# A two-layer hybrid trunk in fp32: one moving operand for twenty more units, the scan's values in one PSUM bank, and the scan branch's gates ahead of its projections

## The chip, the cores and the metric

The kernel runs on one core of a Trainium2 chip. The metric is the time of one execution in device microseconds (us). The matrix engine is called PE (its weight loads PEld), the vector engine DVE, the scalar engine ACT, the general-purpose engine POOL, and SP is the engine that issues most transfers.

## The reference, cut to what matters

Two layers work on a residual stream of 256 tokens by 1024 channels. In each layer one input projection of the normalised stream feeds three token mixers (a state-space scan, attention in a sliding window with sinks and rotary positions, and forgetting attention); each has its own gate path and projection, the results are merged by sigmoid gates and projected back.

```python
h = rms_norm(x, norm_w[layer])
proj = jnp.einsum('bsd,de->bse', h, w_in[layer])
(a_xbc, a_z, a_dt, b_q, b_k, b_v, b_z,
 c_q, c_k, c_v, c_f, c_z, gates) = jnp.split(proj, split_at, axis=-1)
y_a = mamba2_branch(a_xbc, a_z, a_dt, ...)        # 4 groups of 4 heads, chunks of 128 tokens
y_b = sliding_window_branch(b_q, b_k, b_v, b_z, sinks[layer], cos, sin)
y_c = forgetting_attention_branch(c_q, c_k, c_v, c_f, c_z, f_bias[layer])
branch = jnp.einsum('bsiw,iwd->bsid', jnp.stack([y_a, y_b, y_c], axis=2), w_proj[layer])
g = jax.nn.sigmoid(gates.reshape(b, s, N_BRANCH, d) + gate_bias[layer])
x = x + jnp.einsum('bsd,de->bse', jnp.sum(g * branch, axis=2), w_out[layer])
```

Inside the scan branch, after the scan: `y = y + d_skip * xh`, then `y * silu(z)`, then an RMS norm over four groups of 256 channels. The sliding branch rotates q and k by `rope`. All inputs and the output are fp32.

## The kernel before, in words

**Precision.** Every dense product is made of three products of split operands: high by high, low by high, high by low. Weights arrive by SP's queue as `raw` tiles (6 buffers); ACT rounds them to `hi` (line 264) and DVE subtracts to get `lo` (line 265), four parts ahead of PE. The tokens `hT` stand split in the same way, transposed, with high and low side by side.

**Dense units.** A unit makes 128 output channels for all 256 tokens. There are two forms. `chan` (line 443) issues, for each of the 8 slices of the contraction, three matmuls of 256 columns into the same 256 columns of one PSUM bank. `chan_sum` (line 450) issues one of 512 columns, with high and low tokens as one moving operand, and one of 256 for the low weights; the two halves of the bank are then added by an ACT copy (line 463) and a DVE addition (line 464). `tok` makes token-major outputs for gates and projections.

**Who uses which form.** In `rotated` (line 499), which makes the rotary halves of k and q for the sliding branch, all units use `chan`, and DVE multiplies its PSUM result twice, by cosine and sine (line 508); POOL combines the halves (line 517). In `u_z` (line 807), the gate paths, branch 2 uses `chan_sum`, branches 0 (scan) and 1 (sliding) use `chan`.

**Background work.** Attention and scan are generators. `launch` puts one in a list with a delay, and after each dense unit `pump` runs the steps that are due by a planner's clock, within a budget, so that a run of small matmuls stands between two dense units. The constants `D_...` are these delays. PE's order is thus fixed as written; the order on DVE, ACT and POOL is a scheduler's. Dense units use 3 PSUM banks (`mm`), background work 5 (`mx`). A quad of attention heads takes four `mx` banks for its scores, then softmax, transposes of the probabilities (line 594) with ACT copies (line 599), then the product with v.

**The scan** (`ssd_group`, line 739; four groups per layer) has a last phase in which the values are made: for two chunks and two channel blocks, four outputs of 128 by 128, each in an `mx` bank of its own, each followed by a DVE operation that adds the skip term and writes the scan's output (line 801). Before it come the state product (copied by ACT, line 783) and two score products, by which DVE multiplies the decays (line 788). After it the generator waits `D_EVAC` and then returns a token that lets a later generator of the same kind start.

**The scan's group norm** (`group_norm`, line 844; four per layer) sums squares by a matmul with ones, computes the factor on DVE and POOL (line 852), writes it on the diagonals of two tiles by ACT (`diagonals`, line 867, four operations of 128 by 128), waits `D_GN2`, and broadcasts it with two matmuls (line 880). For the first three groups the diagonals are put in a list (`ends_later`), for the last they are written at once.

**The end of a layer** alternates units of gates (`gates_proj`, line 1163; `u_gate`, line 956, adds the bias and takes tanh) and of projections (`u_proj2`, line 990); `merge` (line 1002) takes a gate tile out of `y.gate` and multiplies. For branch 0 the order was four gate-path units, then gates 0, projection 0, gates 1, projection 1.

**SBUF** tiles come from pools by size: `L1` (256 fp32 per partition, 14 buffers), `L2` (512, 7 buffers), `L8` (2048).

Of the kernel before, what the change touches and what calls it, by code (L numbers as in the profile page):

```python
# [16 lines left out]
P = 128  # L17
# [5 lines left out]
EPS = 1e-6  # L23

D_SOFT, D_SOFT2, D_EVAC, D_SSD, D_SSD2 = 7.0, 3.0, 3.0, 8.0, 3.0
D_K, D_Q, D_QK, D_G0, D_FOX, D_BDMA, D_BIAS, D_BC = 6.0, 5.5, 2.0, 8.0, 0.0, 4.0, 2.6, 5.5
D_GN1, D_GN2, D_CUM, D_H, D_M = 6.0, 7.2, 12.0, (4.8, 6.4), 5.0
BUDGET = 1.35
T_PP, T_SSD, T_BIAS = 1, 1, 1
N_RAW, N_SPLIT = 6, 6  # L30
# [14 lines left out]
def hybrid_trunk(  # L45
# [29 lines left out]
    def pmx():  # L75
        return PS("mx", 5)
# [26 lines left out]
    def launch(br, gen, delay=0.0):  # L103
        clock["n"] += 1
        waiting.append([clock["t"] + delay, clock["n"], br, gen, None])
# [390 lines left out]

    def rotated(y, done):

        held = {}

        def u(half):
            def f(w):
                p = chan(y, w, half * P)
                for i in (half, 1 - half):
                    m = held[half, i] = T("L1", [P, S])
                    tt(halves(m), p, halves(cs[:, i, :]), op=ALU.mult)
                if half == 1:
                    done(held)  # L510
                pump()
            return f
        return u(0), u(1)
# [6 lines left out]
    def u_bk(y):  # L520

        def done(held):
            y.kT = T("L8", [P, 4, 2, S])
            add_rotated(y.kT[:, 0, :, :], held)
            for d in range(1, 4):
                m = 32 * d
                nc.gpsimd.dma_start(y.kT[m:P, d, :, :], y.kT[0:P - m, 0, :, :])
                nc.gpsimd.dma_start(y.kT[0:m, d, :, :], y.kT[P - m:P, 0, :, :])
        return rotated(y, done)

    def u_bq(y, g):

        def done(held):
            q = T("qt", [P, 2, S])
            add_rotated(q, held)
            launch(1, swa_quad(y, g, q), D_Q)
        return rotated(y, done)

    def attn_quad(pair, products, biases, nsink, v, vcols, sz, gated, scored=lambda: None):

# [198 lines left out]
    def ssd_group(y, g):  # L739
        yield lambda: not any(m[2] == 1 for m in waiting)  # L740
        yield "bcg"
        bcg = T("L4", [P, 4, S])
        nc.scalar.dma_start(bcg, y.cumd[4 * g:4 * g + 4, 0, :].partition_broadcast(P))
        yield D_BC
        yield "ssd"
        xdt = T("L2", [P, 2, 256])
        hs = slice(4 * g, 4 * g + 4)
        for t in range(2):
            p = pmx()
            for j in range(2):  # L750
                transpose(p[:, j * P:(j + 1) * P], y.xs[:, 2 * g + j, t * P:(t + 1) * P], ident)
            tt(xdt[:, t, :].rearrange("p (h d) -> p h d", h=4),
               p[:, 0:256].rearrange("p (h d) -> p h d", h=4), bc(y.dt[:, t, hs], 2, 64), op=ALU.mult)
        p = pmx()
        transpose(p[:, 0:P], y.bcT[:, g, 0:P], ident)
        bt = T("bt", [P, P])
        act(bt, p[:, 0:P], AF.Copy)
        ds = T("ds", [P, 4], bufs=2)
        tt(ds, bcg[:, :, P - 1], y.acum[:, 0, hs], op=ALU.subtract)
        act(ds, ds, AF.Exp)  # L760
        xds = T("L1", [P, 256])
        tt(xds.rearrange("p (h d) -> p h d", h=4), xdt[:, 0, :].rearrange("p (h d) -> p h d", h=4),
           bc(ds, 2, 64), op=ALU.mult)
        decs = []
        for c in range(2):
            tk = slice(c * P, (c + 1) * P)
            dec = T("L2", [P, 4, P])
            for h in range(4):
                stt(dec[:, h, :], bcg[:, h, tk], y.acum[:, c, 4 * g + h:4 * g + h + 1], negtri,  # L769
                    op0=ALU.subtract, op1=ALU.add)  # L770
            act(dec, dec, AF.Exp)
            decs.append(dec)

        cx = T("L2", [P, 4, P])
        act(cx, bcg[:, :, P:S], AF.Exp)
        tt(cx, cx, bc(y.bcT[:, 4 + g, P:S], 1, 4), op=ALU.mult)
        yield D_SSD
        tokens["bcg"] += 1

        p = pmx()  # L780
        mm(p[:, 0:256], bt, xds, start=True, stop=True)
        st = T("st", [P, 256])
        act(st, p[:, 0:256], AF.Copy)
        for c in range(2):
            tk = slice(c * P, (c + 1) * P)
            p = pmx()
            mm(p[:, 0:P], y.bcT[:, g, tk], y.bcT[:, 4 + g, tk], start=True, stop=True)
            tt(decs[c], decs[c], bc(p[:, 0:P], 1, 4), op=ALU.mult)
        yield D_SSD2
        for c in range(2):  # L790
            tk = slice(c * P, (c + 1) * P)
            for j in range(2):
                u = 2 * g + j
                py = pmx()
                for s in range(c + 1):
                    for i in range(2):
                        h = 2 * j + i
                        hc = slice(64 * h, 64 * h + 64)
                        a, b = (xdt[:, c, hc], decs[c][:, h, :]) if s == 0 else (st[:, hc], cx[:, h, :])
                        mm(py[64 * i:64 * i + 64, 0:P], a, b, start=(s == 0), stop=(s == c))  # L800
                stt(y.xs[:, u, tk], y.xs[:, u, tk], y.dsk[:, u:u + 1], py[:, 0:P],  # L801
                    op0=ALU.mult, op1=ALU.add)
        yield D_EVAC
        tokens["ssd"] += 1


    def u_z(y, br, u, c):
        def f(w):
            if u == 0 and br != 0:
                y.sz[br] = T("L8", [P, NK, S])  # L810
            if br == 2:
                o = y.sz[br][:, u, :]
                chan_sum(y, w, c, o)
                th = T("L1", [P, S])
                act(th, o, AF.Tanh, scale=0.5)
                y.zdone.add((br, u))
                stt(o, th, 1.0, o, op0=ALU.add, op1=ALU.mult)
                pump()
                return
            p = chan(y, w, c)  # L820
            if u == 0 and br == 0:
                y.yh[br] = T("L8", [P, 2, NK, P], F32R)
                y.yl[br] = T("L8", [P, 2, NK, P], F32R)
            th = T("L1", [P, S])
            finish(act(halves(th), p, AF.Tanh, scale=0.5))
            y.zdone.add((br, u))
            if br != 0:
                stt(halves(y.sz[br][:, u, :]), halves(th), 1.0, p, op0=ALU.add, op1=ALU.mult)
            else:
                drain(0)  # L830
                sz = T("L1", [P, S])
                stt(halves(sz), halves(th), 1.0, p, op0=ALU.add, op1=ALU.mult)
                tt(y.xs[:, u, :], y.xs[:, u, :], sz, op=ALU.mult)  # L833
                sq = T("L1", [P, S])
                act(sq, y.xs[:, u, :], AF.Square)
                y.sq.append(sq)
                if u % 2 == 1:
                    tt(y.sq[-2], y.sq[-2], y.sq[-1], op=ALU.add)

                    launch(3 if u < 4 else 4, group_norm(y, u // 2, y.sq[-2]), D_GN1 - (u == 7))  # L840
            pump()
        return f

    def group_norm(y, g, q0):
# [22 lines left out]
                    act(rb[:, t * P:(t + 1) * P], ident, AF.Copy, scale=v[:, 2 * t:2 * t + 1])  # L867


        if g < 3:  # L870
            ends_later.append(diagonals)
        else:
            diagonals()
        yield D_GN2
        if diagonals in ends_later:
            ends_later.remove(diagonals)
# [79 lines left out]
    def u_gate(y, br, c, t):  # L956

        def f(w):
            if t == 0:
                y.gb = T("L2", [P, 512])  # L960
                nc.scalar.dma_start(y.gb, gate_bias[y.l, br:br + 1, c:c + 512].to_broadcast([P, 512]))
            p = tok(y.hTh, y.hTl, w, t)
            g = T("L2", [P, 512])
            tt(halves(g), p, halves(y.gb), op=ALU.add)  # L964
            finish(act(g, g, AF.Tanh, scale=0.5))  # L965
            y.gate[t] = g
            pump()
        return f

# [30 lines left out]
        return f  # L1000

    def merge(y, br, c, t, p, keep=lambda f: f):
        g = y.gate.pop(t)
        m = y.mg[:, t, c:c + 512]
        if br == 1:
            stt(halves(m), halves(g), 1.0, p, op0=ALU.add, op1=ALU.mult)
        else:
            if br == 0:
                stt(halves(g), halves(g), 1.0, p, op0=ALU.add, op1=ALU.mult)
                gtt(m, m, g, op=ALU.add)  # L1010
            else:
                with tc.high_priority():
                    keep(stt)(halves(g), halves(g), 1.0, p, op0=ALU.add, op1=ALU.mult)
                    keep(tt)(m, m, g, op=ALU.add)
                launch(7 + t, mT(y, c, t), D_M)
# [120 lines left out]
    for y in layers:  # L1136
# [26 lines left out]
        def gates_proj(br):  # L1163
# [12 lines left out]
                    op(i, u_proj(y, br, c, 0), u_proj(y, br, c, 1))  # L1176
            seq = [(g, 0), (p, 0), (g, 1), (p, 1)]
            if br == 0:
                seq = [(lambda b: z1(C_ZA, 0, b), b) for b in range(4)] + seq
            return [lambda f=f, b=b: f(b) for f, b in seq]  # L1180

        if l == 0:
# [258 lines left out]
```

## Time and profile before

| | |
|---|---|
| median of 3 runs | 834.85 us (834.35 to 835.0) |
| profiled execution | 834.93 us |
| its span | 833.2 us |
| PE busy | 819.1 us (98%), 5941 matmuls |
| PEld busy | 748.3 us (90%) |
| DVE busy | 670.1 us (80%), 1482 instructions |
| ACT busy | 514.7 us (62%), 1062 instructions |
| POOL busy | 107.3 us (13%) |
| granted PE clock | 0.999 of full speed |

In a row of the timeline come the start in us, the length in us of what the row stands for, the engine, the line of the program, the operation, output and inputs by the program's names, the size, and `xN`, the number of instructions that it joins. In brackets stands how long the engine was idle before it and what ended that. In a row of the groups come busy time in us and the mean of one in ns. In a row of the waits come the total in us, the number of times and the longest. `L` stands for any tile of the pools L1 to L8, `pp` for softmax probabilities, `qt` for rotated or plain queries, `L97` is the helper that issues every matmul, `L101` the one that issues transposes.

### The profile page before, as it was taken

How to read it: one execution, taken by the hardware profiler on the slowest of the kernel's cores; microseconds unless marked ns; L12 is line 12 of the kernel's file. 1: busy time of each engine (PE TensorE's matmuls, PEld its weight loads, DVE VectorE, ACT ScalarE, POOL GpSimd, SP SyncE). 2: the span in 40 equal slices, each digit the busy share in tenths (PEclk: the TensorE clock that was granted, in tenths of full speed). 3: DMA queues.
4: the chain of work that ended last, by engine and by line, in shares of the span. 5: the costliest groups of instructions: out<-in, count | busy, mean ns of one | idle time of the engine just before them, and what ended most of it. 6: DMA issues, size and time to landing. Idle time of an engine off the chain costs nothing.

```text
span 833.2 us, 16124 instructions
## 1 busy us (share of the span) xinstructions
PE 819.1 (98%) x5941; PEld 748.3 (90%) x5941; DVE 670.1 (80%) x1482; ACT 514.7 (62%) x1062; POOL 107.3 (13%) x150
## 2 busy tenths in 40 slices
PE   8999999999999999999999999999999999999996
PEld 7999999988888998888999999989888889888896
DVE  6978998897987787865787789988889778786665
ACT  7747777665766676353564586766646667755442
POOL 3330010100111210210004200001002210121000
PEclk9999999999999999999999999999999999999999
DMA  9975554877656545776689455757776655476632
GB/s 298 273 208 166 174 164 148 241 214 222 173 156 187 169 140 164 246 237 201 209 262 264 133 166 177 205 162 215 230 202 178 176 157 156 133 238 216 215 102 75
DMA packets 129560, 159.41 MB, mean 191 GB/s; under 512 B 7970, under 2 KB 98202, under 8 KB 129482
## 3 DMA queue, kind: packets, MB, share of 16 engines
q1 hardware_dynamic: 114960, 140.53, 55.6%
q10 hardware_dynamic: 13690, 16.24, 6.5%
q0 software_dynamic: 832, 1.62, 0.7%
q8 instruction: 47, 0.77, 0.4%
q14 instruction: 31, 0.25, 0.1%
HBM read 154.63 MB, written 2.16 MB: 188 GB/s over the span
## 4 chain that ended last, share of the span: by engine, by line
PE 50%; DVE 6%; ACT 3%; issue 2%; POOL 1%; ACTq 0%; POOLq 0%; DVEq 0%
PE mm L97 45%; PE mx L97 3%; DVE lo L265 2%; PE mx L101 2%; ACT pp L568 1%; ACT L L867 1%; POOL sm L852 0%; ACT hi L264 0%; DVE pp L580 0%; DVE pp L562 0%; DVE L L833 0%; DVE L L259 0%; DVE L L769 0%; ACT L L599 0%; DVE lo L259 0%
## 5 line engine op out<-in xcount | busy, mean ns | idle before, releaser
L265 DVE TENSOR_TENSOR lo<-raw,hi 128x1024 fp32r<-128x1024 f32 (+2 forms) x276 | 313.5, 1154 | 66.4 <-ACT hi L264 56.7
L97 PE MATMUL mm<-L,hi 128*128 128x256 f32 (+1 forms) x1728 | 365.0, 302 | 0.0
L264 ACT ACTIVATE hi<-raw 128x1024 fp32r<-128x1024 f32 (+2 forms) x276 | 264.6, 980 | 96.3 <-PE mm L97 84.3
L97 PE MATMUL mm<-hi,L 128*128 128x512 f32 (+2 forms) x1232 | 323.7, 351 | 0.2
L97 PEld LDWEIGHTS mm<-L,hi 128*128 128x128 f32 x1728 | 278.4, 191 | 14.0 <-issue 3.4
L97 PE MATMUL mm<-L,lo 128*128 128x256 f32 x1056 | 281.7, 274 | 0.0
L97 PEld LDWEIGHTS mm<-hi,L 128*128 128x128 f32 x1232 | 216.9, 190 | 24.9 <-DVE L L265 1.0
L97 PE MATMUL mm<-lo,L 128*128 128x512 f32 (+2 forms) x616 | 213.6, 348 | 0.0
L97 PEld LDWEIGHTS mm<-L,lo 128*128 128x128 f32 x1056 | 202.5, 192 | 1.9
L97 PEld LDWEIGHTS mm<-lo,L 128*128 128x128 f32 x616 | 116.3, 190 | 11.5
L934 POOL TENSOR_SCALAR_AFFINE_SELECT bias<-bias 128x128 f32<-128x128 f32 x64 | 37.8, 626 | 397.2 <-DMA bias<-cumd 397.2
L568 ACT ACTIVATE pp<-pp,nm 128x128 f32<-128x128 f32 (+1 forms) x128 | 56.6, 444 | 19.0 <-DVE nm L562 19.0
L718 DVE SCALAR_TENSOR_TENSOR L<-L,vec,L 128x255 f32<-128x255 f32 (+2 forms) x96 | 46.1, 481 | 6.6 <-ACT L L715 5.2
L965 ACT ACTIVATE L<-L 128x512 f32<-128x512 f32 x24 | 15.1, 631 | 42.7 <-DVE L L964 42.7
L580 DVE TENSOR_SCALAR pp<-pp,rsum 128x128 f32<-128x128 f32 (+1 forms) x128 | 32.2, 315 | 0.5
L101 PE MATMUL mx<-ident,pp 128*128 128x128 f32 x192 | 27.4, 275 | 3.2 <-DVE L L801 3.2
L599 ACT ACTIVATE L<-mx 128x512 f32<-128x512 f32 x48 | 26.9, 594 | 0.0
L101 PEld LDWEIGHTS mx<-ident,pp 128*128 128x128 f32 x192 | 21.7, 141 | 5.4 <-DVE L L801 4.2
L722 ACT ACTIVATE L<-L 128x256 f32<-128x256 f32 x32 | 13.3, 417 | 20.8 <-DVE L L718 12.5
L562 DVE CUSTOM_DVE_ANT_0 pp<-mx,wmask,nsink 128x128 f32<-128x128 f32 x64 | 23.4, 413 | 1.4 <-PE mx L97 1.4
L568 ACT ACTIVATION_READ_ACCUMULATOR pp<-pp,nm 128x1 f32 x128 | 23.9, 187 | 0.0
L1010 POOL TENSOR_TENSOR L<-L,L 128x512 f32<-128x512 f32 x8 | 15.9, 1994 | 61.7 <-ACT hi L264 32.3
(202 smaller groups left out, 748.9 us busy)
## 6 DMA issues: line engine op xcount, KB each, us to landing
raw<-in_w_in_dram SPq DMA_DIRECT2D x191, 512.0 KB, 4.7
raw<-in_w_proj_dram SPq DMA_DIRECT2D x48, 512.0 KB, 5.4
raw<-in_w_out_dram SPq DMA_DIRECT2D x16, 512.0 KB, 5.5
bias<-cumd ACTq DMA_DIRECT2D x16, 256.0 KB, 4.0
L<-cumd ACTq DMA_DIRECT2D x8, 512.0 KB, 4.6
L<-in_gate_bias_dram ACTq DMA_DIRECT2D x12, 256.0 KB, 3.4
raw<-in_w_in_dram SPq DMA_DIRECT2D x4, 408.0 KB
raw<-in_w_in_dram SPq DMA_DIRECT2D x4, 384.0 KB
```

Of the source, the lines that this page charges most:

```text
L97: nc.tensor.matmul(o, a, b, **kw)
L101: nc.tensor.transpose(o, a, i)
L264: keep(act)(hi, src, AF.Copy)
L265: keep(tt)(lo, src, hi.bitcast(F32), op=ALU.subtract)
L562: nc.vector.tensor_tensor_reduce(out=pp[:, i, sl], in0=score(p, i, b), in1=biases(p, i, b), scale=-0.125, scalar=1.0e30 if ns is None else ...
L568: act(pp[:, i, sl], pp[:, i, sl], AF.Exp, scale=-1.0, bias=nm[:, e:e + 1], accum_out=sums[:, e:e + 1])
L580: ts(pp[:, i, sl], pp[:, i, sl], rs[:, 2 * i + b:2 * i + b + 1], 0.5, op0=ALU.mult, op1=ALU.mult)
L599: act(pT, pt, AF.Copy)
L718: stt(a[:, s:S], x_[:, 0:S - s], y.vec[:, 16 * j + u:16 * j + u + 1], a[:, s:S], op0=ALU.mult, op1=ALU.add)
L934: nc.gpsimd.affine_select(out=bias[:, i, dst], in_=bias[:, i, src], compare_op=ALU.is_ge, fill=NEG, base=0, pattern=[[-1, P]], channel_mul ...
L965: finish(act(g, g, AF.Tanh, scale=0.5))
L1010: gtt(m, m, g, op=ALU.add)
```

## The change

Three edits, with the delays that belong to them.

1. `rotated` gets a switch `both`; with it the unit goes through `chan_sum` into an `L1` tile and the two multiplications read that tile. It is on for query groups 1 to 3, off for group 0 and for k. `u_z` uses `chan_sum` also for branch 1 with `u < 4`.
2. The values of a scan group go into one bank: all products first, then two DVE operations of 256 columns in place of four of 128. The token comes back after `D_SSD3` = 1.0 in place of `D_EVAC` = 3.0.
3. In branch 0 both gate units come before both projection units, gate tiles are kept by column block and token block, all groups' diagonals go into the list, the first delay is the same for all groups, and `D_GN2` goes from 7.2 to 9.0.

```diff
-D_GN1, D_GN2, D_CUM, D_H, D_M = 6.0, 7.2, 12.0, (4.8, 6.4), 5.0
+D_GN1, D_GN2, D_CUM, D_H, D_M = 6.0, 9.0, 12.0, (4.8, 6.4), 5.0      # and D_SSD3 = 1.0
...
-    def rotated(y, done):
+    def rotated(y, done, both):
...
-                p = chan(y, w, half * P)
+                if both:
+                    p = T("L1", [P, S])
+                    chan_sum(y, w, half * P, p)
+                    p = halves(p)
+                else:
+                    p = chan(y, w, half * P)
...
-        return rotated(y, done)                # k
+        return rotated(y, done, False)
...
-        return rotated(y, done)                # q of group g
+        return rotated(y, done, g > 0)
...
         yield D_SSD2
+        py = pmx()
         for c in range(2):
-            tk = slice(c * P, (c + 1) * P)
             for j in range(2):
-                u = 2 * g + j
-                py = pmx()
+                o = py[:, S * j + P * c:S * j + P * c + P]
                 for s in range(c + 1):
                     for i in range(2):
...
-                        mm(py[64 * i:64 * i + 64, 0:P], a, b, start=(s == 0), stop=(s == c))
-                stt(y.xs[:, u, tk], y.xs[:, u, tk], y.dsk[:, u:u + 1], py[:, 0:P],
-                    op0=ALU.mult, op1=ALU.add)
-        yield D_EVAC
+                        mm(o[64 * i:64 * i + 64, :], a, b, start=(s == 0), stop=(s == c))
+        for j in range(2):
+            u = 2 * g + j
+            stt(y.xs[:, u, :], y.xs[:, u, :], y.dsk[:, u:u + 1], py[:, S * j:S * j + S], op0=ALU.mult, op1=ALU.add)
+        yield D_SSD3
...
-            if br == 2:
+            if br == 2 or br == 1 and u < 4:
...
-                    launch(3 if u < 4 else 4, group_norm(y, u // 2, y.sq[-2]), D_GN1 - (u == 7))
+                    launch(3 if u < 4 else 4, group_norm(y, u // 2, y.sq[-2]), D_GN1)
...
-        if g < 3:
-            ends_later.append(diagonals)
-        else:
-            diagonals()
+        ends_later.append(diagonals)
...
-            y.gate[t] = g
+            y.gate[c, t] = g
...
-        g = y.gate.pop(t)
+        g = y.gate.pop((c, t))
...
             if br == 0:
-                seq = [(lambda b: z1(C_ZA, 0, b), b) for b in range(4)] + seq
+                seq = [(lambda b: z1(C_ZA, 0, b), b) for b in range(4)] + [(g, 0), (g, 1), (p, 0), (p, 1)]
```

More of the change, by code (lines that the diff above doesn't have):

```diff
@@ L25 @@
 D_SOFT, D_SOFT2, D_EVAC, D_SSD, D_SSD2 = 7.0, 3.0, 3.0, 8.0, 3.0
-D_K, D_Q, D_QK, D_G0, D_FOX, D_BDMA, D_BIAS, D_BC = 6.0, 5.5, 2.0, 8.0, 0.0, 4.0, 2.6, 5.5
-D_GN1, D_GN2, D_CUM, D_H, D_M = 6.0, 7.2, 12.0, (4.8, 6.4), 5.0
+D_K, D_Q, D_QK, D_G0, D_FOX, D_BDMA, D_BIAS, D_BC, D_SSD3 = 6.0, 5.5, 2.0, 8.0, 0.0, 4.0, 2.6, 5.5, 1.0
+D_GN1, D_GN2, D_CUM, D_H, D_M = 6.0, 9.0, 12.0, (4.8, 6.4), 5.0
 BUDGET = 1.35
```

## The prediction, made before the changed kernel ran

> **What bounds the kernel now.** I read the first part of the profile page, then the waits view, and from there the timeline at the places that it names.
>
> ```profile
> span 833.2 us, 16124 instructions
> PE 819.1 (98%) x5941; PEld 748.3 (90%) x5941; DVE 670.1 (80%) x1482; ACT 514.7 (62%) x1062; POOL 107.3 (13%) x150
> PE mx L101 <- DVE L L801: 3.2, 4, 1.1
> PEld mx L97 <- ACT L L867: 2.4, 4, 0.8
> ```
>
> TensorE (PE) is busy for 98% of the span, so the time moves only with what PE has to do and with the few places where it stands still. Two of those places belong to this change: four waits of PE for line 801, the evictions of the scan's values (3.2 us in total, the longest 1.1), and four weight loads that wait for line 867, the diagonals of the scan branch's group norm. VectorE (DVE), at 80%, is the next engine; what is given to it must be watched.
>
> The profiled execution took 834.93 us, 1.73 more than its span, and the median of the runs is 834.85. The sum starts from 834.93; the two differ by 0.08, which is nothing here. I use 0.2% (1.7 us) as what a measurement of this kernel can tell from no change.
>
> **Twenty units with one operand.** A unit with `chan` issues 24 matmuls of 256 columns; one with `chan_sum` issues 8 of 512 and 8 of 256. Both forms already stand in the trace, in undisturbed stretches:
>
> ```profile
> 60.80 0.28 PE L97 MATMUL mm<-L,lo 128*128 128x256 f32 x1
> ...
> 66.16 0.28 PE L97 MATMUL mm<-L,lo 128*128 128x256 f32 x1
> 225.00 0.38 PE L97 MATMUL mm<-L,hi 128*128 128x512 f32 x1
> ...
> 226.97 0.38 PE L97 MATMUL mm<-L,hi 128*128 128x512 f32 x1
> ```
>
> In the first stretch 16 triples start within 66.16 − 60.80 = 5.36 us, 0.335 each, so eight triples, one unit, take 2.68 us. In the second, six pairs start within 1.97 us, 0.328 each, so a unit takes 2.62. The switch saves 0.06 us, because a column costs PE the same in either form and only eight starts are saved. The change switches 6 query units (groups 1 to 3, two each) and 4 gate units per layer, 20 in both layers: **−1.2 us**.
>
> [...]
>
> What the form adds runs on ACT and DVE:
>
> ```profile
> L463 ACT ACTIVATE qt<-mm 128x256 f32<-128x256 f32 x32 | 12.1, 377 | 16.4 <-PE mm L97 16.2
> L464 DVE TENSOR_TENSOR qt<-mm,qt 128x256 f32<-128x256 f32 x32 | 13.4, 419 | 2.9 <-ACT qt L463 2.5
> L508 DVE TENSOR_TENSOR L<-mm,cs 128x256 f32<-128x256 f32 x40 | 14.9, 413 | 0.6 <-PE mm L97 0.6
> 28.00:56.00 28.00, 28.00 (x251) 27.80 (x250) 25.13 (x42) 15.98 (x30) 11.70 (x15) 1.00 0.86 240
> 56.00:75.00 19.00, 19.00 (x190) 18.53 (x189) 14.81 (x46) 12.13 (x36) 3.14 (x6) 1.00 0.49 143
> ```
>
> Each unit gets one L463 (377 ns) and one L464 (419 ns). The PSUM bank is not held longer: it was read by two L508 of 413 ns, and now by 377 + 419. In the query stage (28 to 56 us) DVE is busy for 25.13 of 28 us and six more instructions bring 6 × 0.419 = 2.5 us per layer. That just fits into the 2.87 us left, and the weight splits stand ahead of PE by some units, so I take 0; without that cover it costs up to 2.5 per layer. The four gate units add 4 × 0.419 = 1.7 us per layer in the stage after it, where DVE is busy for 14.81 of 19 us: 0. (In both rows the columns are the stretch and its length, then the busy time of PE, PEld, DVE, ACT and POOL.)
>
> **The scan's values in one bank.** Each group now takes one bank where it took four, and two evictions of 256 columns where it made four of 128. What that ends can be seen where the transposes of a softmax follow the values in one run:
>
> ```profile
> 228.74 0.66 PE L101 MATMUL mx<-ident,pp 128*128 128x128 f32 x4
> 229.50 0.59 DVE L801 SCALAR_TENSOR_TENSOR L<-L,dsk,mx 128x128 f32<-128x128 f32 x2
> 229.89 0.44 PE L101 MATMUL mx<-ident,pp 128*128 128x128 f32 x2 [0.50 <-DVE L L801]
> 251.23 0.66 PE L101 MATMUL mx<-ident,pp 128*128 128x128 f32 x4
> 253.03 0.44 PE L101 MATMUL mx<-ident,pp 128*128 128x128 f32 x2 [1.14 <-DVE L L801]
> 636.98 0.66 PE L101 MATMUL mx<-ident,pp 128*128 128x128 f32 x4
> 638.13 0.44 PE L101 MATMUL mx<-ident,pp 128*128 128x128 f32 x2 [0.50 <-DVE L L801]
> 659.48 0.66 PE L101 MATMUL mx<-ident,pp 128*128 128x128 f32 x4
> 661.21 0.44 PE L101 MATMUL mx<-ident,pp 128*128 128x128 f32 x2 [1.07 <-DVE L L801]
> ```
>
> There are five banks for this work. The values hold four, the first four transposes take the fifth, and the last two need a bank that only L801 frees. Four transposes in 0.66 us, of which the last one's end is some 0.14 behind its pitch, set the next start at about +0.51. The fifth transpose started 1.15, 1.80, 1.15 and 1.73 us after the first: lost are 0.64, 1.29, 0.64 and 1.22, together **−3.8 us**. After the change the two generators also end up in different runs of PE (in the changed order no transposes follow the values directly), and even together they would need three banks. Both reasons take the wait away.
>
> The evictions get cheaper too. By the rows
>
> ```profile
> L801 DVE SCALAR_TENSOR_TENSOR L<-L,dsk,mx 128x128 f32<-128x128 f32 x32 | 9.2, 339 | 0.0
> L883 DVE SCALAR_TENSOR_TENSOR L<-L,vec,mx 128x256 f32<-128x256 f32 x16 | 6.9, 472 | 0.0
> ```
>
> 32 × 339 ns become 16 × 472: DVE gives back 3.3 us of what it got, off the path.
>
> [...]
>
> The delay before the group's token is given falls from 3.0 to 1.0. That lets later generators start sooner; what they run into is the first rival.
>
> **Gates first in the scan branch.** Both gate units now precede both projection units, the second delay of the group norm grows from 7.2 to 9.0, and the last group's diagonals are queued like the others. Before, two groups' broadcast products stood in one run, which stopped for the diagonals:
>
> ```profile
> 320.68 0.38 PE L97 MATMUL mm<-lo,L 128*128 128x512 f32 x1
> 321.47 0.39 PE L97 MATMUL mx<-L,ones 128*128 128x256 f32 x1 [0.41 <-ACT L L867]
> 322.05 0.62 PE L97 MATMUL mx<-L,ones 128*128 128x256 f32 x3 [0.20 <-ACT L L867]
> 728.84 0.38 PE L97 MATMUL mm<-lo,L 128*128 128x512 f32 x1
> 729.64 0.38 PE L97 MATMUL mx<-L,ones 128*128 128x256 f32 x1 [0.42 <-ACT L L867]
> 730.22 0.63 PE L97 MATMUL mx<-L,ones 128*128 128x256 f32 x3 [0.20 <-ACT L L867]
> ```
>
> From the start of the last dense matmul (its pitch is 0.22, read off 225.00 to 226.97 with 0.11 for the 256-column one) the first product should have come at 320.90 and 729.06. It came 0.57 and 0.58 late, and the next one 0.47 late again both times (0.58 instead of 0.11): 1.04 + 1.05 = **−2.1 us**. In the changed order every group's broadcast stands apart, at least one dense unit behind its own diagonals; that unit lasts over 2 us, the eight diagonals in two rows of 1.55 and 0.97 us about 2.5, and there are at least three units between the sums and the broadcast. The projections lose nothing, since they come two gate units later and their operand is ready sooner than needed. Four gate tiles live at once, which with the biases just fills the seven buffers of that size; the price if a gate unit had to wait for one is in the range.
>
> **Sum.** −1.2 − 3.8 − 2.1 = −7.1 us: 834.93 − 7.1 = **827.8 us**. Splitting the four joint runs adds a few switches, some tenths at most, and the runs without a wait are a little shorter than reckoned; I let these cancel.
>
> **The rivals.** First, a new wait takes the place of the old one. In the changed order four runs (groups 2 and 3, both layers) hold the scan's state product and its two score products directly ahead of a fox quad's scores. These take three banks, the scores four, so the third and fourth score bank wait for the copy of the state (L783) and the first L788. In the trace of before the same products were read late:
>
> ```profile
> 216.83 1.58 PE L97 MATMUL mx<-qt 64*128 64x128 f32 x16
> 221.06 0.59 PE L97 MATMUL mx<-L,bt 128*128 128x256 f32 x2
> 223.41 0.37 ACT L783 ACTIVATE st<-mx 128x256 f32<-128x256 f32 x1
> 223.46 0.68 DVE L788 TENSOR_TENSOR L<-L,mx 128x512 f32<-128x512 f32 x1
> 243.56 0.59 PE L97 MATMUL mx<-L,bt 128*128 128x256 f32 x2
> 246.39 0.36 ACT L783 ACTIVATE st<-mx 128x256 f32<-128x256 f32 x1
> 246.78 1.28 DVE L788 TENSOR_TENSOR L<-L,mx 128x512 f32<-128x512 f32 x2
> 250.75 1.22 DVE L265 TENSOR_TENSOR lo<-raw,hi 128x1024 fp32r<-128x1024 f32 x1
> ```
>
> The scores use a bank per 0.4 us (1.58 for four). The state and score products end some 0.8 us after 221.06, so a third bank would be wanted at about 222.7 and was free at 223.78 (1.1 late); in the other, wanted at 245.2, free at 246.75, and the fourth at 247.42 (1.7 late in all). With those lags the four runs cost 2 × 2.8 = 5.6 us and the time is 833.4, the gain nearly eaten. Against it: in both places L783 and L788 stood behind a softmax that was then in its queue; in the changed order only weight splits and one L464 precede them, and by their durations (at most 1.22 + 0.42 + 0.68 from the last score product) the wait is a few tenths, if any. I give the lags of before 0.12.
>
> Second, the slower side: the same wait, with one more weight split of 1.22 us ahead of L788 each time (DVE is busy for 80% of the span). Then the four cost 2 × (2.3 + 2.9) = 10.4, and the time is 838.2. It turns to slower by 0.2% from (7.1 + 1.7)/4 = 2.2 us per run on. 0.06, and 0.04 more for a wait of that size elsewhere.
>
> Third, DVE becomes the bound of the query stage and PE stands for all that was added: 2 × 2.5 = 5.0 us, 832.8. Against: the row above has just enough room. 0.07.
>
> Fourth, the change doesn't do what it says: the waits for banks and diagonals move a run further instead of going. Only the dense part stays: 833.7. The changed order speaks against it: 0.06.
>
> [...] The 48 units of that form in the trace run at 2.62: 0.01.
>
> **How the numbers follow.** The forecast has 0.64, between 826.2 (each of the eight stops also costs a weight load that otherwise runs beside a matmul, 748.3/5941 = 0.13 each and 1.0 in all, and the relief of DVE is worth some tenths) and 830.5 (the new bank waits at half their lags). The range of 826.2 to 833.2 takes in the third rival and half of the first; left out are the second, the fourth, the fifth and the other half, about 0.2. Faster by over 0.2% means under 833.2: 0.64 + 0.07 + 0.01 + half of 0.12 + most of what lies between, 0.82; same, the fourth and the rest of the first, 0.08; slower 0.10.
>
> **What would show it.** Right: no wait of PE for L801 or L867; 5781 matmuls instead of 5941; `chan_sum` units at 0.328 a pair; DVE near 670 + 5.0 + 3.4 − 3.3 = 675 us; the waits view of PE without those two names. Wrong: waits of PE for L783 or the changed L788 over 1 us (the first two rivals), waits of the query stage's matmuls for L265 (the third), or PE waiting for the diagonals again, now with a projection behind it.

## The result, and the profile after

The changed kernel took 830.0 us (median of 5 runs, 829.68 to 830.79) against 834.85 us before (5 runs, 833.68 to 835.57). The ratio is 0.9942, interval 0.993 to 0.9954: faster by 4.8 us, with 3.8 to 5.8 inside the interval. The forecast was 827.8 in a range of 826.2 to 833.2: the direction and the range held, and 2.2 us of the expected gain are missing.

The first part of the page of after:

```profile
span 828.2 us, 15796 instructions
PE 818.4 (99%) x5781; PEld 743.7 (90%) x5781; DVE 676.0 (82%) x1486; ACT 522.7 (63%) x1082; POOL 97.3 (12%) x150
```

The span fell by 5.0 us. PE issues 160 matmuls fewer and its busy time falls by only 0.7: the gain is mostly idle time that went. DVE rose by 5.9 us to 676.0, where the prediction reckoned 675.

The waits view of after, for PE, its weight loads and DVE (total, times, longest):

```profile
PEld mx L97 <- ACT L L872: 1.6, 4, 0.4
PEld mx L97 <- DVE L L793: 1.1, 4, 0.3
PEld mx L97 <- ACT st L788: 0.7, 2, 0.4
PEld mm L97 <- DVE qt L464: 0.6, 1, 0.6
DVE ds L764 <- DMA L<-cumd: 6.8, 2, 3.9
```

(Line numbers are those of the changed kernel: L872 the diagonals, before L867; L808 the scan's evictions, before L801; L793 and L788, before L788 and L783.) The stops for the scan's evictions, the largest of before, are gone. The stops for the diagonals are not: four are left. And three names are new or larger: the two that the joint run of scan products and scores waits for, and one stop for a query eviction. The timeline of after at these places:

```profile
223.50 0.86 DVE L808 SCALAR_TENSOR_TENSOR L<-L,dsk,mx 128x256 f32<-128x256 f32 x2
...
235.17 0.59 PE L97 MATMUL mx<-L,bt 128*128 128x256 f32 x2
235.32 1.23 DVE L265 TENSOR_TENSOR lo<-raw,hi 128x1024 fp32r<-128x1024 f32 x1 [0.88 <-ACT hi L264]
235.65 1.05 ACT L264 ACTIVATE hi<-raw 128x1024 fp32r<-128x1024 f32 x1
236.14 2.31 PE L97 MATMUL mx<-qt 64*128 64x128 f32 x16
236.47 0.42 DVE L464 TENSOR_TENSOR qt<-mm,qt 128x256 f32<-128x256 f32 x1
236.60 0.38 ACT L788 ACTIVATE st<-mx 128x256 f32<-128x256 f32 x1
236.80 1.27 DVE L793 TENSOR_TENSOR L<-L,mx 128x512 f32<-128x512 f32 x2
237.03 0.29 PEld L97 LDWEIGHTS mx<-qt 64*128 64x128 f32 x2 [0.36 <-ACT st L788]
237.53 0.52 PEld L97 LDWEIGHTS mx<-qt 64*128 64x128 f32 x6 [0.21 <-DVE L L793]
...
317.66 0.61 ACT L967 ACTIVATE L<-L 128x512 f32<-128x512 f32 x1
318.18 0.97 ACT L872 ACTIVATE L<-ident,sm 128x128 fp32r<-128x128 f32 x3
318.53 0.38 PE L97 MATMUL mm<-lo,L 128*128 128x512 f32 x1
318.91 0.38 PE L97 MATMUL mx<-L,ones 128*128 128x256 f32 x1
319.06 0.38 ACT L872 ACTIVATE L<-ident,sm 128x128 fp32r<-128x128 f32 x1
319.49 0.39 PE L97 MATMUL mx<-L,ones 128*128 128x256 f32 x1 [0.20 <-ACT L L872]
```

Three things are to be seen. The evictions of the scan's values are two (0.86 us in a row of the two) and nobody waits for them. In the joint run the sixteen score matmuls take 2.31 us, where they took 1.58 before: the third bank waits for the state's copy (L788, 236.60), the fourth for L793 (236.80). On DVE, L793 stands behind a weight split (235.32) and an L464, the very queue that the prediction named; on ACT, the copy stands behind the rounding of a weight (235.65), which it did not name. In the joint run before this one, which loses only 0.06 us, both engines are further along: the copy and the first L793 start 0.63 and 0.96 us after the run's first product, here 1.43 and 1.63 us. And the third group's diagonals start at 318.18, right behind the gate's tanh (L967), while PE is ready for the broadcast at 318.75 (318.53 and that matmul's pitch of 0.22); it gets the two halves at 318.91 and 319.49.

**The account.** From the timeline I took each run of background matmuls, from the last dense matmul ahead of it to the second one behind it, less these matmuls' own pitch, and added up those of a kind:

| kind of run, both layers | before | after |
|---|---|---|
| scan values and softmax transposes, together or apart | 35.5 | 31.7 |
| scan products and scores, together or apart | 20.7 | 22.2 |
| group norm, with what shares its runs | 14.0 | 12.9 |

That is −3.8, +1.6 and −1.1 us (before rounding). Dense units give −1.2 by their pitch, and one stop in layer 1 takes 0.5 back. These come to −4.0. Most of the rest of the 5.0 lies in the start: PE waits there for the input's transfer,

```profile
10.32 0.66 PE L101 MATMUL mx<-ident,L 128*128 128x128 f32 x4 [0.67 <-DMA L<-in_x_dram]
```

in the timeline of before, and in that of after

```profile
9.41 0.65 PE L101 MATMUL mx<-ident,L 128*128 128x128 f32 x4 [0.47 <-DMA L<-in_x_dram]
```

which is 0.9 us earlier. In the profiled executions of the experiments this row starts between 9.1 and 10.5 us, in two executions of one kernel at 10.2 and 10.5. After (9.4) and that kernel differ in one delay of the scan, far behind this row, so I put the difference down to the execution and not to the change. Each profile below is therefore compared by the cost of its runs, and by the medians only where they differ by more than this.

### The profile page after: what moved, and what is told of

It is laid out like the page before. It is cut to its first block, busy times and chain, and to the rows that moved or that the text cites. A ratio compares the mean times of both kernels' runs of the same rounds, so it can differ in the third digit from the quotient of the medians.

```text
span 828.2 us, 15796 instructions
## 1 busy us (share of the span) xinstructions
PE 818.4 (99%) x5781; PEld 743.7 (90%) x5781; DVE 676.0 (82%) x1486; ACT 522.7 (63%) x1082; POOL 97.3 (12%) x150
## 4 chain that ended last, share of the span: by engine, by line
PE 90%; DVE 4%; issue 2%; DMA 2%; ACT 1%; SPq 0%; POOLq 0%; POOL 0%; DVEq 0%; ACTq 0%
PE mm L97 79%; PE mx L97 8%; PE mx L101 4%; DVE lo L265 1%; DMA L<-cumd 1%; DMA L<-in_x_dram 1%; DVE L L723 0%; ACT hi L264 0%; DVE L L265 0%; ACT L L872 0%; DVE pp L567 0%; DVE L L259 0%; DVE L L774 0%; DVE lo L259 0%; DVE pp L585 0%
## 5 line engine op out<-in xcount | busy, mean ns | idle before, releaser
L97 PE MATMUL mm<-L,lo 128*128 128x256 f32 x1056 | 278.3, 274 | 0.0
L97 PEld LDWEIGHTS mm<-L,hi 128*128 128x128 f32 x1568 | 258.5, 191 | 18.1 <-issue 5.1
L97 PEld LDWEIGHTS mm<-lo,L 128*128 128x128 f32 x616 | 116.4, 190 | 11.5
L936 POOL TENSOR_SCALAR_AFFINE_SELECT bias<-bias 128x128 f32<-128x128 f32 x64 | 31.0, 520 | 394.9 <-DMA bias<-cumd 377.3
L463 ACT ACTIVATE L<-mm 128x256 f32<-128x256 f32 x36 | 13.7, 381 | 26.5 <-PE mm L97 26.0
L967 ACT ACTIVATE L<-L 128x512 f32<-128x512 f32 x24 | 15.1, 628 | 20.4 <-DVE L L966 20.4
L966 DVE TENSOR_TENSOR L<-mm,L 128x512 f32<-128x512 f32 x24 | 16.4, 684 | 9.4 <-PE mm L97 8.2
```

Of the source, the lines that this page charges most:

```text
L97: nc.tensor.matmul(o, a, b, **kw)
L936: nc.gpsimd.affine_select(out=bias[:, i, dst], in_=bias[:, i, src], compare_op=ALU.is_ge, fill=NEG, base=0, pattern=[[-1, P]], channel_mul ...
```

## The experiments

My theory after the result: the scan's stops went as forecast, the delay of 1.0 brought the joint runs and their waits, and the third group's diagonals come too late in the new order.

**e1: the first edit alone**, twenty units with one operand on the kernel before.

```diff
+ rotated(..., both) and u_z with chan_sum for br == 1 and u < 4, as in the change
```

> The kernel before with only the first edit: the twenty units with one operand. Order of PE's background work as before. Theory: a unit goes from 2.68 to 2.62 us and nothing else moves: 834.85 - 1.2 = 833.6, with the four stops for line 801 (3.2 us in the waits) and the four for the diagonals still there. If the wait of 0.5 us behind the query eviction that the changed kernel shows in layer 1 comes from the extra DVE work of this edit, it stands here too, and the time is 834.1. Rival (DVE bounds the query stage): about 838, with matmuls of that stage waiting for the weight splits.

Measured: 833.76 us, ratio 0.9985 (0.9976 to 0.9995), 0.4 to 2.0 us less. The waits view of e1 (here L806 is the eviction and L872 the diagonals):

```profile
PE mx L101 <- DVE L L806: 3.1, 4, 1.2
PEld mx L97 <- ACT L L872: 2.4, 4, 0.8
PEld mm L97 <- DVE qt L464: 2.0, 4, 0.7
DVE ds L764 <- DMA L<-cumd: 9.9, 4, 4.8
```

The old stops stand as before, PE waits no more for weight splits than before (its weight loads 1.3 + 1.0 us in both), and a pair of 512 and 256 columns takes 0.328 us in this trace too (six from 151.39 to 153.36). So the 1.2 us are there, and the rival in which DVE bounds that stage is out. The stop for the query eviction is here too, longer than in after, as it should be if this edit's work on DVE caused it; e2 and e5b show another cause.

**e2: the second edit alone**, one bank and the delay of 1.0 on the kernel before.

```diff
+ py = pmx() once per group, two evictions of 256 columns
- yield D_EVAC          # 3.0
+ yield D_SSD3          # 1.0
```

> The kernel before with only the second edit: one bank for the scan's values and the delay of 1.0 before the token. Theory: the four stops for line 801 go (-3.9), and the four joint runs of scan products and scores come in with their waits (+1.6, the third and fourth at 3.31 us, the other two at 2.64): 832.5 less what the group norm gains because its broadcasts stand apart in this order, 0 to 2.1: 830.4 to 832.5. Rival (the joint runs are harmless, their waits come from the other edits): 828.9 to 831.

Measured: 835.37 us, ratio 1.0004 (0.9992 to 1.0016): nothing gained, outside what I expected. The stops for the evictions are gone, but the waits view has others:

```profile
PEld mx L97 <- ACT L L868: 3.9, 4, 1.5
PEld mx L97 <- DVE L L788: 3.2, 5, 2.3
```

and its timeline, in layer 1,

```profile
179.82 0.16 DVE L759 TENSOR_TENSOR ds<-L,acum 128x4 f32<-128x4 f32 x1 [1.93 <-DMA L<-cumd]
182.56 1.03 PE L97 MATMUL mx<-L,L 128*64 128x128 f32 x12 [1.87 <-DVE L L788]
```

Two of the group norm's broadcasts, with the delay of 7.2, now come so close behind their diagonals that each costs 2.1 us where an undisturbed one costs 0.24 (before, two joint ones cost 1.6 each). The joint runs cost 2.64, 2.64, 3.23 and 3.37, +1.5 us, as in after. And in layer 1 the first group's values waited 2.1 us for L788, because DVE had stood at L759 for a transfer of the third group's decays, issued 7.2 us before that. Layer 2 has no such wait, and this profile (837.19 us) is 1.8 above the median; how many of the timed runs have it is open. I had counted the group norm as a gain or nothing; it was a loss.

**e3: one bank with the old delay.**

```diff
- yield D_SSD3          # 1.0
+ yield D_EVAC          # 3.0, e2's kernel otherwise
```

> The second edit with the old delay of 3.0 before the token: one bank in place of four and nothing else; the runs of PE keep the composition of the kernel before, values and softmax transposes together, no joint run with scores. If the number of banks takes the stop away: four runs of about 2.3 us in place of 2.98 to 3.63, -3.9, 830.9. If it is the shorter delay, which separates values and transposes, that takes it away: 834.8.

Measured: 831.34 us, ratio 0.9949 (0.9936 to 0.9962). Timeline of e3, the transposes behind the values:

```profile
228.67 0.88 PE L101 MATMUL mx<-ident,pp 128*128 128x128 f32 x6
229.44 0.86 DVE L803 SCALAR_TENSOR_TENSOR L<-L,dsk,mx 128x256 f32<-128x256 f32 x2
```

All six transposes go in one row of 0.88 us, which starts ahead of the evictions. The four runs cost 2.27 us each in place of 2.98 to 3.63: −4.1 us from the number of banks alone. In four banks the values held what the next work needed: before, the transposes stopped four times for L801 (3.2 us in total), and in e3 they do not stop at all.

**e4: the third edit alone.**

```diff
+ seq of branch 0: (g, 0), (g, 1), (p, 0), (p, 1); D_GN2 9.0; all diagonals in ends_later
```

> The kernel before with only the third edit: gates of the scan branch first, delay 9.0, all diagonals in the list. The last group's broadcast now stands three units behind its sums, where the changed kernel has it two units behind. Theory: no stop for the diagonals, -2.1, 832.8, with the four stops for line 801 untouched. Rival (the stop is moved by the gates' order to the last group whatever the distance, as the changed kernel shows 0.7 per layer): 833.8.

Measured: 831.74 us, ratio 0.9962 (0.9949 to 0.9974). Timeline of e4:

```profile
311.47 0.48 PE L97 MATMUL mx<-L,ones 128*128 128x256 f32 x2
316.50 0.63 ACT L962 ACTIVATE L<-L 128x512 f32<-128x512 f32 x1 [1.38 <-DVE L L961]
317.04 1.26 ACT L867 ACTIVATE L<-ident,sm 128x128 fp32r<-128x128 f32 x4
322.59 0.40 PE L97 MATMUL mx<-L,ones 128*128 128x256 f32 x2
```

The third group's diagonals come 0.54 us behind the start of a gate's tanh (L962) and are done at 318.30; the broadcast comes at 322.59: no stop. All background runs together cost 117.4 us in place of 120.7. Of these 3.3 us the group norm's runs make 2.3; 0.7 is the stop for the input at the start, which this execution does not have. So the edit is worth 2.3 us where the third group's broadcast stands further behind that tanh, 6.1 us here; in the changed kernel, where PE is ready for it 1.1 us behind, it gave 1.1.

**e5: the changed kernel with the scan's delay back at 3.0**, and **e5b**, the same kernel again.

```diff
- D_SSD3 = 1.0
+ D_SSD3 = 3.0
```

> The changed kernel with the delay before the scan's token back at 3.0 (one number). Runs of values and transposes are together again, but with one bank; no scores behind the scan's products; the last broadcast of the group norm falls one unit later. Theory: the joint runs' cost goes (-1.6), so does the last stop for the diagonals (-1.4), and one bank is enough to keep the transposes going: 830.0 - 3.0 = 827.0. Rival (the shorter delay is what took the stop for line 801 away): +3.9 instead, 830.9.

> The kernel of e5 once more, on the same chip as e9: 828.1, and 826.8 if the transfer lands within 6.6 us of its issue in the profiled execution and in most others.

Measured: 828.08 us, ratio to before 0.9909 (0.9893 to 0.9924); again: 827.24 us, 0.9904 (0.9888 to 0.992). All four joint runs are gone, the four runs of values and transposes cost 2.27 each, and no broadcast waits; the background runs cost 114.1 us (114.7 the second time, with a stop for the input that is 0.6 longer) against 117.2 in after. One number gives back what the change lost. What is left in e5 are two stops in layer 1, each for a query eviction; the timeline at the first:

```profile
150.85 0.97 ACTq L748 DMA_DIRECT2D L<-cumd  x2
158.68 0.16 DVE L764 TENSOR_TENSOR ds<-L,acum 128x4 f32<-128x4 f32 x1 [4.94 <-DMA L<-cumd]
159.90 0.42 DVE L464 TENSOR_TENSOR qt<-mm,qt 128x256 f32<-128x256 f32 x1
160.38 0.48 PE L97 MATMUL mm<-L,hi 128*128 128x512 f32 x1 [0.57 <-DVE qt L464]
```

In e5b there is none:

```profile
151.17 0.95 ACTq L748 DMA_DIRECT2D L<-cumd  x2
156.75 0.16 DVE L764 TENSOR_TENSOR ds<-L,acum 128x4 f32<-128x4 f32 x1 [2.69 <-DMA L<-cumd]
157.98 0.42 DVE L464 TENSOR_TENSOR qt<-mm,qt 128x256 f32<-128x256 f32 x1
```

DVE stands at L764 until a transfer of the scan's decays has landed, and the query eviction stands behind it. In e5 DVE goes on 7.8 us after the issue and PE loses 1.3 us there (two stops); in e5b 5.6 us after it, and PE loses nothing. Over the ten profiles with L764 (before: L759) at this place on DVE: when DVE goes on 5.4 to 6.1 us after the issue (before, e3, e4, e5b, e7), PE has no stop there in layer 1; with 6.8 to 7.8 (after, e1, e2, e6, e5) it has one. Kernels with the first edit and kernels without it are on both sides, and so is one kernel run twice: this stop belongs to when that transfer lands. It is not what the change's DVE work costs.

**e6: the changed kernel with four banks again.**

```diff
- py = pmx() once per group, two evictions
+ py = pmx() for each of four values, four evictions
```

> The changed kernel with four banks and four evictions for the scan's values as before, all else kept (delay 1.0 too). If the order alone keeps transposes away from the values, nothing waits for four banks: 830.0, and DVE has 3.3 us more to do. If the one bank is what matters: 833.9, with stops for the evictions.

Measured: 831.91 us, ratio to before 0.9959 (0.9946 to 0.9973), between the two expectations. No run is stopped by an eviction, since in this order no transposes follow the values: the order alone takes the old stops away, as the bank count alone does in e3. But PE waits longer in the joint run (timeline of e6):

```profile
236.91 1.23 DVE L265 TENSOR_TENSOR lo<-raw,hi 128x1024 fp32r<-128x1024 f32 x1 [0.87 <-ACT hi L264]
238.42 0.29 PEld L97 LDWEIGHTS mx<-qt 64*128 64x128 f32 x2 [0.42 <-ACT st L788]
239.12 0.52 PEld L97 LDWEIGHTS mx<-qt 64*128 64x128 f32 x6 [0.40 <-DVE L L793]
```

The two longer joint runs cost 3.56 and 3.63 in place of 3.31, and all runs together 0.9 us more than in after. DVE's added work is not seen to be the reason: DVE stands idle for 0.87 us ahead of the weight split that L793 follows, until ACT has rounded that weight. Against the run's first product that split starts at 0.40 us here and at 0.15 in after; why ACT is later is open. The transfer of the decays landed after 7.0 us and cost stops as in e1.

**e7: the changed kernel with the group norm's second delay at 12.0.**

```diff
- D_GN2 = 9.0
+ D_GN2 = 12.0
```

> The changed kernel with the second delay of the group norm at 12.0 in place of 9.0: the last broadcast stands one unit further behind its sums. Theory: the last stop for the diagonals goes (0.72 us per layer in two products), the joint runs stay: 830.0 - 1.4 = 828.6. Rival (the diagonals are held by the queue of ACT, behind roundings, and come as late again): 830.0.

Measured: 829.18 us, ratio to before 0.9931 (0.9917 to 0.9945). Timeline of e7:

```profile
316.65 1.26 ACT L872 ACTIVATE L<-ident,sm 128x128 fp32r<-128x128 f32 x4
321.30 0.40 PE L97 MATMUL mx<-L,ones 128*128 128x256 f32 x2
```

The broadcasts that cost 0.96 and 0.97 us in after cost 0.24 each, and the background runs 115.4 in place of 117.2 (0.3 of it at the start); the joint runs stay at 2.64, 2.64, 3.31 and 3.38. The diagonals again come right behind the gate's tanh, 0.52 us after its start at 316.13, but the broadcast 5.2 us after it. The distance from that tanh is what decides: PE is ready for the broadcast 11.5 us behind the third group's sums both in after, with the stop, and in e4, without.

**e8: e5 with the scan's steps one unit later**, and **e9: e5 with line 764 on POOL**, two attempts on the stop for the transfer.

```diff
- D_BC = 5.5
+ D_BC = 8.0                                      # e8
- tt(ds, bcg[:, :, P - 1], y.acum[:, 0, hs], op=ALU.subtract)
+ gtt(ds, bcg[:, :, P - 1], y.acum[:, 0, hs], op=ALU.subtract)   # e9
```

> The changed kernel with the delay before the scan's token at 3.0 and the delay between the transfer of the cumulated decays and the scan group's first step at 8.0 in place of 5.5; the scan's steps stand one unit later in PE's order, and the transposes come ahead of the values in the joint runs. Theory: DVE no longer stands 2.5 to 4.9 us for that transfer at the first group, so the query eviction behind it is not late and PE's two stops of together 1.3 us there go: 828.1 - 1.3 = 826.8. Rival (the eviction is late because DVE is full at that place, not because of the transfer): 828.1 with the same stops one unit later, or more where the scan's last group now falls on the gates.

Measured: 826.97 us, ratio to before 0.9906 (0.9893 to 0.992), the lowest median, not distinguishable from e5b. The time came out as expected but not for my reason: DVE still stands 3.7 us for the transfer. This landing (6.6 us from the issue) might have cost nothing in e5 either, so whether the delay helps stays open.

> The changed kernel with delay 3.0 (as in e5) and the small subtraction of line 764, on which DVE stood 2.5 to 4.9 us for the transfer of the decays, given to POOL. The order on PE is the same. Theory (the query evictions are late because DVE stands in line behind that transfer): no stop of PE for the query eviction in layer 1 however late the transfer lands, 0.6 to 1.3 us under e5 where e5 has the stops, none where it hasn't: 826.8 to 828. Rival (DVE is full there for other reasons): the stops stay. If POOL, busy with the masks of line 936, comes to the subtraction late, the scan's products wait instead, and the time is over 829.

Measured: 828.07 us, ratio to before 0.9918 (0.9905 to 0.9931); no gain. PE waits for a query eviction twice in each layer (2.0 us in all), which the theory had ruled out for layer 1. Timeline of e9:

```profile
156.63 0.21 ACT L765 ACTIVATE ds<-ds 128x4 f32<-128x4 f32 x1 [3.24 <-POOL ds L764]
570.28 0.36 ACT L463 ACTIVATE qt<-mm 128x256 f32<-128x256 f32 x1
573.27 0.41 DVE L464 TENSOR_TENSOR qt<-mm,qt 128x256 f32<-128x256 f32 x1
573.83 0.35 PE L97 MATMUL mm<-L,hi 128*128 128x256 f32 x1 [0.82 <-DVE qt L464]
```

DVE no longer stands for the transfer. But the next instruction of that chain, an exponential on ACT (L765), needs POOL's result, and now ACT stands: 3.24 us at the first group of layer 1, 0.83 at the second group of each layer. The convolution's copies stand behind it on ACT, DVE waits 0.82 us for these copies and then works without a stop; a query that ACT copied at 570.28 is finished by DVE only from 573.27 on, and PE stops. Moving one instruction of a chain to another engine moved the place of the wait. In layer 1 the transfer was used 6.4 us after its issue, between the times that cost nothing and those that cost a stop, so this run does not test a late landing.

## Why the prediction was right or wrong, point by point

- **Dense units, −1.2: right.** e1 measured 0.4 to 2.0 us, and the pair takes the 0.328 us that the prediction read off. No run shows a cause for the fifth rival's 0.01: the pair takes 0.328 us in before and in e1.
- **The scan's stops, −3.8: right in size.** It gave both reasons, and e3 and e6 show that each suffices: one bank with the old order costs 2.27 us a run, four banks with the new order show no such stop.
- **Evictions at 472 ns: right.** The groups view of after has

```profile
L808 DVE SCALAR_TENSOR_TENSOR L<-L,dsk,mx 128x256 f32<-128x256 f32 x16 | 6.9, 475 | 1.6 <-PE mx L97 1.6
```

- **The group norm, −2.1: half wrong, 1.1.** The failed step is "In the changed order every group's broadcast stands apart, at least one dense unit behind its own diagonals". It counted the units between sums and broadcast, but not that the diagonals in the list are issued only behind the next gate's tanh, and that ACT had roundings and that tanh before them. Apart was right; behind its diagonals was not. e4 and e7 show the full gain once the broadcast stands 5 to 6 us behind that tanh in place of 1.1.
- **Splitting and switches, "I let these cancel": wrong, +1.6.** This was the first rival in a mild form. The prediction's bound for it (a split, an L464 and L788 ahead) was the queue that occurred on DVE (on ACT a rounding came on top, ahead of the state's copy), but it was put down as "a few tenths, if any"; two runs cost 0.73 us each above their parts, and the other two 0.06. In e5 these runs stand apart again and the cost is gone. The price with the lags of before, 5.6, was too high by three and a half times, since no softmax stood in these queues, as argued.
- **DVE as the bound of the query stage: did not come.** e1 has no stop in that stage.
- **What nobody forecast, +0.5 and −0.9:** the query eviction behind the late transfer, and the start of the profiled execution. Both vary between executions of one kernel.

By these the forecast's −7.1 becomes −4.0 without the start, inside the interval of 3.8 to 5.8 less. That the time fell into the range is owed to the room left for new bank waits; a loss at the diagonals stood only in its fourth rival, which the range left out. In e5, where neither the joint runs nor the late diagonals stand, the forecast's sum comes out: 828.1 and 827.2 against 827.8. How much of the 0.8 us up to the medians' difference is the start in the timed runs is open.

## What to carry to other kernels

A shorter delay in a hand-written order moves what stands next to what; list which pieces share a run before and after, and count the banks of each such run against the evictions that free them. For every wait that should vanish, check the full chain of its producer, with the queue in which it is issued: a distance in units from the sums said nothing about diagonals that are only issued behind another unit's tanh. When an edit bundles a resource and a delay, try them apart: here one number of the bundle (3.0 in place of 1.0) was worth 1.9 to 2.8 us by the medians, about a third of the forecast gain.

## What the runs showed of the hardware that I had not expected

A transfer of 512 KB, issued at the same place in the program, was used by DVE, which stood waiting for it, between 5.4 and 7.8 us after its issue, in two executions of one kernel at 5.6 and 7.8; from 6.8 us on PE stopped there in layer 1. The first rows of PE that wait for the input also move by up to 1.4 us. Differences of a microsecond between single profiles of this kernel can be that alone.

A multiplication on DVE did not get cheaper when its input moved from PSUM to SBUF. The groups of after:

```profile
L513 DVE TENSOR_TENSOR L<-L,cs 128x256 f32<-128x256 f32 x24 | 9.5, 434 | 0.6
L513 DVE TENSOR_TENSOR L<-mm,cs 128x256 f32<-128x256 f32 x16 | 6.0, 414 | 0.6 <-PE mm L97 0.6
```

From SBUF (`L`) it takes 434 ns in the mean, from PSUM (`mm`) 414. Four of the 24 from SBUF took 505 to 516 ns; the medians are 422 and 414. By the medians the multiplication takes 8 ns more from SBUF in this trace.
